# Batch norm with ReLU on one core: the stores of two neighbouring 4 MB pieces made one transfer from one tile

The kernel runs on one NeuronCore of a Trainium2 chip (the other cores stay idle). The metric is the device time of one execution in microseconds (us), where lower is better. The "span" of a profile is a little shorter: it was 81.9 us in a run of 83.77 us. The pieces of 1, 2, 4 and 8 MB are counted in units of 1024 x 1024 bytes, so a piece of 4 MB is 4.19 of the profile's MB.

## The reference, cut to what matters

```
x: (32, 128, 32, 32) float32;  gamma, beta, running_mean, running_var: (128,) float32;  eps = 1e-5
normalized = (x - running_mean[c]) / sqrt(running_var[c] + eps)
out = maximum(normalized * gamma[c] + beta[c], 0)          # float32
```

Every element is read once (16.78 MB) and written once (16.78 MB). With scale = gamma / sqrt(var + eps) and bias = beta - mean x scale, the arithmetic is one activation, relu(scale x + bias), for each row of a channel.

## The kernel before

The (batch, channel) rows are laid out as two halves (t = 0, 1) of 128 partitions with 16 rows of 1024 elements (4 KB) in each partition. A partition's 16 rows lie next to each other in memory (64 KB), and the halves lie 8 MB apart. Each piece has a block of on-chip memory, a tile. SyncE loads the pieces, ACT (ScalarE) activates them in place, and ACT issues the stores:

```python
PIECES = (((0, 2), (2, 4), (4, 8), (8, 16)), ((0, 8), (8, 16)))
STORE_CUTS = {(0, 1)}
...
for t in range(T):
    for a, b in PIECES[t]:
        xt = data.tile([P, b - a, HW], F32, name=f"x{t}_{a}")
        nc.sync.dma_start(out=xt, in_=xr[t, :, a:b, :])
        tiles.append((t, a, b, xt))
# ... four tiny parameter loads on ACT's queue, then scale_t and bias_t [P, 16] (cut)
for t, a, b, xt in tiles:
    first = a
    for j in range(a, b):
        nc.scalar.activation(out=xt[:, j - a, :], in_=xt[:, j - a, :], func=ACTF.Relu,
                             bias=bias_t[:, j : j + 1], scale=scale_t[:, j : j + 1])
        if j + 1 == b or (t, j + 1) in STORE_CUTS:
            nc.scalar.dma_start(out=outr[t, :, first : j + 1, :],
                                in_=xt[:, first - a : j + 1 - a, :])
            first = j + 1
```

So there are six loads (1, 1, 2, 4, 4, 4 MB) and seven stores (0.5, 0.5, 1, 2, 4, 4, 4 MB).

Of the kernel before, what the change touches and what calls it, by code (L numbers as in the profile page):

```python
# [1 line left out]

# [4 lines left out]


F32 = mybir.dt.float32
ACTF = mybir.ActivationFunctionType  # L10



J = 16

PIECES = (((0, 2), (2, 4), (4, 8), (8, 16)), ((0, 8), (8, 16)))

STORE_CUTS = {(0, 1)}


@with_exitstack
def kernel(
    ctx: ExitStack,
    tc: tile.TileContext,
    x: bass.AP,
    gamma: bass.AP,
    beta: bass.AP,
    running_mean: bass.AP,
    running_var: bass.AP,
    eps: bass.AP,  # L30
    out: bass.AP,
):
    nc = tc.nc
    B, C, H, W = x.shape
    HW = H * W
    P = nc.NUM_PARTITIONS
    assert C % J == 0 and P % (C // J) == 0 and (B * C) % (P * J) == 0
    Q = C // J
    T = B * C // (P * J)

    xr = x.rearrange("b c h w -> (b c) (h w)").rearrange("(t p j) w -> t p j w", p=P, j=J)
    outr = out.rearrange("b c h w -> (b c) (h w)").rearrange("(t p j) w -> t p j w", p=P, j=J)

    data = ctx.enter_context(tc.tile_pool(name="data", bufs=1))
    params = ctx.enter_context(tc.tile_pool(name="params", bufs=1))
    psum = ctx.enter_context(tc.tile_pool(name="psum", bufs=1, space=bass.MemoryType.PSUM))

    tiles = []
    for t in range(T):
        for a, b in PIECES[t]:  # L50
            xt = data.tile([P, b - a, HW], F32, name=f"x{t}_{a}")
            nc.sync.dma_start(out=xt, in_=xr[t, :, a:b, :])  # L52
            tiles.append((t, a, b, xt))



    raw = params.tile([Q, 4, J], F32, name="raw")
    for k, src in enumerate((running_var, gamma, running_mean, beta)):
        nc.scalar.dma_start(out=raw[:, k, :], in_=src.rearrange("(q j) -> q j", j=J))
    eps_t = params.tile([P, 1], F32, name="eps_t")  # L60
    nc.vector.memset(eps_t, float(eps))  # L61
    rep = params.tile([Q, P // Q, Q], F32, name="rep")
    nc.gpsimd.memset(rep, 1.0)  # L63
    nc.gpsimd.affine_select(  # L64
        out=rep,
        in_=rep,
        compare_op=mybir.AluOpType.is_equal,
        fill=0.0,
        base=0,
        pattern=[[0, P // Q], [-1, Q]],  # L70
        channel_multiplier=1,
    )
    cols = psum.tile([P, 4, J], F32, name="cols")
    nc.tensor.matmul(  # L74
        cols.rearrange("p k j -> p (k j)"),
        rep.rearrange("q r s -> q (r s)"),
        raw.rearrange("q k j -> q (k j)"),
        start=True,
        stop=True,
    )  # L80
    std_t = params.tile([P, J], F32, name="std_t")
    nc.scalar.activation(out=std_t, in_=cols[:, 0, :], func=ACTF.Sqrt, bias=eps_t[:, 0:1], scale=1.0)  # L82
    rstd_t = params.tile([P, J], F32, name="rstd_t")
    nc.vector.reciprocal(out=rstd_t, in_=std_t)  # L84
    scale_t = params.tile([P, J], F32, name="scale_t")
    nc.vector.tensor_mul(out=scale_t, in0=cols[:, 1, :], in1=rstd_t)  # L86
    ms_t = params.tile([P, J], F32, name="ms_t")
    nc.vector.tensor_mul(out=ms_t, in0=cols[:, 2, :], in1=scale_t)  # L88
    bias_t = params.tile([P, J], F32, name="bias_t")
    nc.vector.tensor_sub(out=bias_t, in0=cols[:, 3, :], in1=ms_t)  # L90

    with tc.manual_schedule(engines={mybir.EngineType.Activation}):
        for t, a, b, xt in tiles:
            first = a
            for j in range(a, b):
                nc.scalar.activation(  # L96
                    out=xt[:, j - a, :],
                    in_=xt[:, j - a, :],
                    func=ACTF.Relu,
                    bias=bias_t[:, j : j + 1],  # L100
                    scale=scale_t[:, j : j + 1],
                )
                if j + 1 == b or (t, j + 1) in STORE_CUTS:
                    nc.scalar.dma_start(
                        out=outr[t, :, first : j + 1, :], in_=xt[:, first - a : j + 1 - a, :]
                    )
                    first = j + 1


# [1 line left out]
_INS = ['x', 'gamma', 'beta', 'running_mean', 'running_var', 'eps']  # L111
_OUTS = [((32, 128, 32, 32), 'float32')]

_NUMBERS = {'eps': 1e-05}


# [26 lines left out]
```

## Time and profile before

| | before |
|---|---|
| time, median of the first 3 runs | 83.94 us (83.83 to 84.08) |
| span of the profiled run | 81.9 us |
| ACT busy | 38.5 us, 47% |
| packets of loads + packets of stores and parameters, share of the 16 DMA engines | 48.4% + 47.8% |
| bytes | 33.56 MB, 410 GB/s over the span |

The share of the DMA engines is the number to read first: the two queues together fill 96% of the span. The prediction below shows these lines and reads them.

### The profile page before, as it was taken

How to read it: one execution, taken by the hardware profiler on the slowest of the kernel's cores; microseconds unless marked ns; L12 is line 12 of the kernel's file. 1: busy time of each engine (PE TensorE's matmuls, PEld its weight loads, DVE VectorE, ACT ScalarE, POOL GpSimd, SP SyncE). 2: the span in 40 equal slices, each digit the busy share in tenths (PEclk: the TensorE clock that was granted, in tenths of full speed). 3: DMA queues.
4: the chain of work that ended last, by engine and by line, in shares of the span. 5: the costliest groups of instructions: out<-in, count | busy, mean ns of one | idle time of the engine just before them, and what ended most of it. 6: DMA issues, size and time to landing. Idle time of an engine off the chain costs nothing.

```text
span 81.9 us, 119 instructions
## 1 busy us (share of the span) xinstructions
PE 0.7 (1%) x2; PEld 0.5 (1%) x2; DVE 0.8 (1%) x5; ACT 38.5 (47%) x34; POOL 0.8 (1%) x6
## 2 busy tenths in 40 slices
PE   0002000000000000000000000000000000000000
PEld 0002000000000000000000000000000000000000
DVE  0000300000000000000000000000000000000000
ACT  0600377799039999199994199993000000000000
POOL 3000000000000000000000000000000000000000
DMA  2899999989899999979789798996999899799690
GB/s 32 328 425 472 408 448 448 512 352 494 370 448 416 446 418 396 500 296 600 320 380 580 304 464 384 512 512 288 480 512 400 368 512 448 320 512 496 272 512 0
DMA packets 1936, 33.56 MB, mean 410 GB/s; under 512 B 272, under 2 KB 272, under 8 KB 528
## 3 DMA queue, kind: packets, MB, share of 16 engines
q1 hardware_dynamic: 864, 16.78, 48.4%
q10 hardware_dynamic: 1072, 16.78, 47.8%
HBM read 16.78 MB, written 16.78 MB: 410 GB/s over the span
## 4 chain that ended last, share of the span: by engine, by line
DMA 56%; ACT 11%; SPq 0%; issue 0%
DMA x<-in_x_dram 56%; ACT x L96 11%; SPq L52 0%
## 5 line engine op out<-in xcount | busy, mean ns | idle before, releaser
L96 ACT ACTIVATE x<-x,bias_t,scale_t 128x1024 f32<-128x1024 f32 x32 | 37.0, 1228 | 10.3 <-DMA x<-in_x_dram 7.9
L82 ACT ACT_TABLE_LOAD x1 | 1.3, 1283 | 2.6 <-issue 2.6
L82 ACT ACTIVATE std_t<-cols,eps_t 128x16 f32<-128x16 f32 x1 | 0.3, 273 | 4.5 <-PE cols L74 4.5
L74 PE MATMUL cols<-raw,rep 8*128 8x64 f32 x2 | 0.7, 428 | 7.7 <-DMA raw<-in_beta_dram 7.7
L74 PEld LDWEIGHTS cols<-raw,rep 8*128 8x128 f32 x2 | 0.5, 304 | 7.7 <-issue 7.7
L64 POOL TENSOR_SCALAR_AFFINE_SELECT rep<-rep 8x128 f32<-8x128 f32 x1 | 0.4, 392 | 0.1
L84 DVE RECIPROCAL rstd_t<-std_t 128x16 f32<-128x16 f32 x1 | 0.3, 254 | 7.8 <-ACT std_t L82 7.8
L63 POOL MEMSET rep<- 8x128 f32 x1 | 0.2, 195 | 0.3 <-POOLq L124 0.3
L86 DVE TENSOR_TENSOR scale_t<-cols,rstd_t 128x16 f32<-128x16 f32 x1 | 0.2, 175 | 0.1
L90 DVE TENSOR_TENSOR bias_t<-cols,ms_t 128x16 f32<-128x16 f32 x1 | 0.2, 175 | 0.0
L88 DVE TENSOR_TENSOR ms_t<-cols,scale_t 128x16 f32<-128x16 f32 x1 | 0.2, 175 | 0.0
L124 POOL MEMSET const-bfloat16-1.0<- 128x1 bf16 x1 | 0.1, 106 | 0.0
L124 POOL MEMSET const-uint8-127<- 128x1 uint8 x1 | 0.1, 106 | 0.0
L124 POOL MEMSET const-float32-0.0<- 128x1 f32 x1 | 0.1, 103 | 0.3 <-issue 0.3
L124 POOL MEMSET const-float32-1.0<- 128x1 f32 x1 | 0.1, 103 | 0.0
L61 DVE MEMSET eps_t<- 128x1 f32 x1 | 0.1, 59 | 0.9 <-PEq L124 0.9
## 6 DMA issues: line engine op xcount, KB each, us to landing
x<-in_x_dram SPq DMA_DIRECT2D x3, 4096.0 KB, 38.8
out_dram<-x ACTq DMA_DIRECT2D x3, 4096.0 KB, 27.9
x<-in_x_dram SPq DMA_DIRECT2D x2, 1024.0 KB, 5.7
x<-in_x_dram SPq DMA_DIRECT2D x1, 2048.0 KB, 11.2
out_dram<-x ACTq DMA_DIRECT2D x1, 2048.0 KB
out_dram<-x ACTq DMA_DIRECT2D x2, 512.0 KB, 18.8
out_dram<-x ACTq DMA_DIRECT2D x1, 1024.0 KB
raw<-in_running_var_dram ACTq DMA_DIRECT2D x1, 0.5 KB
```

Source lines behind the costliest of these rows:

```text
L61: nc.vector.memset(eps_t, float(eps))
L63: nc.gpsimd.memset(rep, 1.0)
L64: nc.gpsimd.affine_select(out=rep, in_=rep, compare_op=mybir.AluOpType.is_equal, fill=0.0, base=0, pattern=[[0, P // Q], [-1, Q]], channel ...
L74: nc.tensor.matmul(cols.rearrange("p k j -> p (k j)"), rep.rearrange("q r s -> q (r s)"), raw.rearrange("q k j -> q (k j)"), start=True, s ...
L82: nc.scalar.activation(out=std_t, in_=cols[:, 0, :], func=ACTF.Sqrt, bias=eps_t[:, 0:1], scale=1.0)
L84: nc.vector.reciprocal(out=rstd_t, in_=std_t)
L86: nc.vector.tensor_mul(out=scale_t, in0=cols[:, 1, :], in1=rstd_t)
L88: nc.vector.tensor_mul(out=ms_t, in0=cols[:, 2, :], in1=scale_t)
L90: nc.vector.tensor_sub(out=bias_t, in0=cols[:, 3, :], in1=ms_t)
L96: nc.scalar.activation(out=xt[:, j - a, :], in_=xt[:, j - a, :], func=ACTF.Relu, bias=bias_t[:, j : j + 1], scale=scale_t[:, j : j + 1],)
L124: nc = _bacc.Bacc("TRN2", target_bir_lowering=False, num_devices=1)
```

## The change

The tile of the first half's rows 8 to 15 and the tile of the second half's rows 0 to 7 become one tile with two parts. Each part is loaded and activated as before, but they are stored by a single transfer after the second part. That makes one transfer, one issue and one completion (a tiny packet on each of the 16 engines, as the packet counts show) less, with larger transfers; in exchange the first part's store is ready later.

```diff
-PIECES = (((0, 2), (2, 4), (4, 8), (8, 16)), ((0, 8), (8, 16)))
-STORE_CUTS = {(0, 1)}
+TILES = (((0, 0, 2),), ((0, 2, 4),), ((0, 4, 8),), ((0, 8, 16), (1, 0, 8)), ((1, 8, 16),))
+STORE_CUTS = {(0, 0)}
...
+    for pieces in TILES:
+        n = len(pieces)
+        rows = pieces[0][2] - pieces[0][1]
+        xt = data.tile([P, n, rows, HW], F32, name=f"x{pieces[0][0]}_{pieces[0][1]}")
+        for i, (t, a, b) in enumerate(pieces):
+            nc.sync.dma_start(out=xt[:, i], in_=xr[t, :, a:b, :])
+        tiles.append((pieces, xt))
...  (activations as before, on xt[:, i, j - a, :]; single pieces are stored as before)
+            if len(pieces) == 2:
+                (t0, a, b), (t1, c, _) = pieces
+                pitch = ((t1 - t0) * P * J + c - a) * HW
+                nc.scalar.dma_start(
+                    out=bass.AP(tensor=outr.tensor, offset=outr[t0, :, a:b, :].offset,
+                                ap=[[J * HW, P], [pitch, 2], [HW, b - a], [1, HW]]),
+                    in_=xt)
```

More of the change, by code (lines that the diff above doesn't have):

```diff
@@ L48 @@
     tiles = []
-    for t in range(T):
-        for a, b in PIECES[t]:
-            xt = data.tile([P, b - a, HW], F32, name=f"x{t}_{a}")
-            nc.sync.dma_start(out=xt, in_=xr[t, :, a:b, :])
-            tiles.append((t, a, b, xt))
+    for pieces in TILES:
[5 more added lines that the diff above has]
+        tiles.append((pieces, xt))
     raw = params.tile([Q, 4, J], F32, name="raw")
@@ L92 @@
     with tc.manual_schedule(engines={mybir.EngineType.Activation}):
-        for t, a, b, xt in tiles:
-            first = a
-            for j in range(a, b):
-                nc.scalar.activation(
-                    out=xt[:, j - a, :],
-                    in_=xt[:, j - a, :],
-                    func=ACTF.Relu,
-                    bias=bias_t[:, j : j + 1],
-                    scale=scale_t[:, j : j + 1],
-                )
-                if j + 1 == b or (t, j + 1) in STORE_CUTS:
-                    nc.scalar.dma_start(
-                        out=outr[t, :, first : j + 1, :], in_=xt[:, first - a : j + 1 - a, :]
-                    )
-                    first = j + 1
+        for pieces, xt in tiles:
+            first = 0
+            for i, (t, a, b) in enumerate(pieces):
+                for j in range(a, b):
+                    nc.scalar.activation(
+                        out=xt[:, i, j - a, :],
+                        in_=xt[:, i, j - a, :],
+                        func=ACTF.Relu,
+                        bias=bias_t[:, j : j + 1],
+                        scale=scale_t[:, j : j + 1],
+                    )
+                    if len(pieces) == 1 and (j + 1 == b or (t, j) in STORE_CUTS):
+                        nc.scalar.dma_start(
+                            out=outr[t, :, a + first : j + 1, :], in_=xt[:, 0, first : j + 1 - a, :]
+                        )
+                        first = j + 1 - a
+            if len(pieces) == 2:
+                (t0, a, b), (t1, c, _) = pieces
+                pitch = ((t1 - t0) * P * J + c - a) * HW
+                nc.scalar.dma_start(
+                    out=bass.AP(
+                        tensor=outr.tensor,
+                        offset=outr[t0, :, a:b, :].offset,
+                        ap=[[J * HW, P], [pitch, 2], [HW, b - a], [1, HW]],
+                    ),
+                    in_=xt,
+                )
 _INS = ['x', 'gamma', 'beta', 'running_mean', 'running_var', 'eps']
```

## The prediction

What the text says of the hardware can be looked up in the trace of the kernel before:

- The 435 GB/s is 4.19 MB in the 9.65 us between the two landings (61.65 and 71.30 us).
- From 24 to 44 us the loads and the stores have 240 packets each, with 7.34 and 1.18 MB.
- The packets of the stores start in the order of the issues: those of 4 KB from 14.6 us, of 8 KB from 36.6, of 16 KB from 46.4 and of 32 KB from 51.2 us. So nothing of the store issued at 33.05 us moved before 51.2 us.
- A completion packet took 0.009 us. A packet of 32 KB took 1.213 us, one of 16 KB 0.611 and one of 4 KB 0.159; eight of 4 KB are 1.27 us, 5% more than one of 32 KB (the text's "some per cent").

> **What bounds the kernel now.** I read the page first (busy shares, the 40 slices, the queue table), then the chain of waits, then the transfers in single stretches of time, then the timeline of ScalarE (ACT). The page:
>
> ```profile
> span 81.9 us, 119 instructions
> ...
> PE 0.7 (1%) x2; PEld 0.5 (1%) x2; DVE 0.8 (1%) x5; ACT 38.5 (47%) x34; POOL 0.8 (1%) x6
> ...
> DMA  2899999989899999979789798996999899799690
> ...
> q1 hardware_dynamic: 864, 16.78, 48.4%
> q10 hardware_dynamic: 1072, 16.78, 47.8%
> HBM read 16.78 MB, written 16.78 MB: 410 GB/s over the span
> ```
>
> ACT, the only busy compute engine, works 47% of the span. The packets of the two queues (q1: the loads, issued by SyncE; q10: the parameters and the stores, issued by ACT) take 48.4 + 47.8 = 96.2% of the time of all 16 DMA engines, 78.8 of 81.9 us. The row of slices shows where the rest is: the first slice (2) and the last two (9, then 0). So the kernel is bound by moving 33.56 MB, and what a change is worth is decided by whether it alters the bytes, the rate, or the time for which the engines stand empty.
>
> The chain that ended last tells less than it seems to:
>
> ```profile
> 7.99 38.77 DMA x<-in_x_dram
> 46.76 0.03 issue
> 46.79 9.16 ACT x L96 x8
> ```
>
> It ends with the last eight activations at 55.95 us, though 26 us of the span are still to come: the stores after them are followed by no instruction, so the chain doesn't count them. It must not be read as "the loads and ACT set the end". The stretches show it. First the timeline of ACT around the two stores concerned, then the queues from 0 to 44 us, from 46.8 to 81.9 us and from 80.5 us on:
>
> ```profile
> 33.05 0.34 ACTq L104 DMA_DIRECT2D out_dram<-x  x1
> 34.81 9.16 ACT L96 ACTIVATE x<-x,bias_t,scale_t 128x1024 f32<-128x1024 f32 x8 [1.79 <-DMA x<-in_x_dram]
> 44.00 0.34 ACTq L104 DMA_DIRECT2D out_dram<-x  x1
> 46.79 9.16 ACT L96 ACTIVATE x<-x,bias_t,scale_t 128x1024 f32<-128x1024 f32 x8 [2.82 <-DMA x<-in_x_dram]
> 55.97 0.34 ACTq L104 DMA_DIRECT2D out_dram<-x  x1
> ```
>
> ```profile
> q1 hardware_dynamic: 832, 16.25, 87.3%
> q10 hardware_dynamic: 432, 1.71, 9.4%
> ```
>
> ```profile
> q10 hardware_dynamic: 560, 14.42, 95.2%
> ```
>
> ```profile
> DMA packets 4, 0.00 MB, mean 0 GB/s; under 512 B 4, under 2 KB 4, under 8 KB 4
> ```
>
> By 44.0 us the stores had moved 1.71 MB, but 4.19 MB of stores (0.52 + 0.52 + 1.05 + 2.10) had been issued by 20.57 us. So 4.19 - 1.71 = 2.48 MB of older stores still stood in front of the store issued at 33.05, not one byte of which can have moved. That store landed at about 33.05 + 28.6 = 61.7 us (28.6 is the longest time to landing among the seven stores), the one of 44.00 at 44.00 + 27.3 = 71.3 us: 9.6 us apart, which is 4.19 MB at 435 GB/s. From 46.8 us on there are only stores, 14.42 MB of them, and the engines are full until the last data packets end before 80.5 us; after that there are four tiny completion packets. The first of the two stores thus starts near 61.7 - 9.7 = 52 us, the second near 61.7, the last near 71.3.
>
> [...] the packet counts are those of one packet for each partition of each transfer and one for each engine's completion (q1: 6 transfers x (128 + 16) = 864; q10: 7 x 144 = 1008, and 4 parameter loads x 16 = 64, together 1072). [...]
>
> [...] 430, 437 and 427 GB/s in the stretches 64 to 72, 72 to 78 and 46.8 to 56 us. [...]
>
> [...]
>
> [...] The merged store writes for each partition two runs of 32 KB that lie 8 MB less 32 KB apart. No run of before shows such a pattern; I take it up as a rival.
>
> **The change part by part.** The loads are the same six transfers in the same order, from the same engine with the same waits; only the destination of two of them is now one tile. The order of the instructions in the built program confirms that. Of the 32 activations none is added or removed; before the 17th to 24th and the 25th to 32nd the waits on their loads stay.
>
> (1) Removed: the store at 33.05 us, 0.34 us of ACT's queue. ACT then waited 1.79 us for a load anyway (until 34.81), so the 0.34 us lie in idle time: 0 us on the path.
>
> (2) Moved: 4.19 MB of store become ready at 44.00 instead of 33.05 us, 10.95 us later. They are not needed before about 52 us, since the queue serves 2.48 MB of older stores first, between 44.0 and 52. Slack: 52 - 44 = 8 us. Cost 0 us.
>
> (3) Merged: an 8.39 MB store at 44.00 with 2 x 128 runs of 32 KB. At 435 GB/s it takes 19.3 us, as the two did (9.6 + 9.6): 0 us. It should land where the second landed, at 71.3 us, with the last store behind it: the last is issued at 55.97 as before, 15 us ahead of its turn.
>
> (4) Completions: one transfer less is one completion packet less on each engine. The completions of before are 17 transfers on 16 or 8 engines, all among the 272 packets under 512 B; even at the whole 3.1 us that the queues leave unused they could not take more than 3.1 / 17 = 0.2 us each, and as tiny packets far less. Estimate, from 4 of them taking 0.2% of the 1.4 us stretch on all 16 engines: 0.002 x 1.4 x 16 / 4 = 0.01 us each. Gain about 0.01 us, and some hundredths more if the two runs of a partition go as one packet.
>
> (5) Waits by reuse of semaphores: the built program has eight for its transfers in turn, so one store less shifts who waits for whom. Before, the store at 44.00 also waited for the very first store; now the last store, at 55.97, does. The first store was issued at 10.99 and landed 14.2 us later, at 25.2 us. 0 us.
>
> The issue of the merged store may take longer than 0.34 us. ACT has 2.82 us of idle before the load of 46.76 is there, so up to 2.4 us more are free. Sum: 0 to -0.1 us on 83.94 us.
>
> **The rivals.** *Starvation*: the store of the first half's last rows leaves 11 us later, and the DMA engines run dry. For it: 4.19 MB are held back in a kernel bound by its transfers. If it happened without any backlog it would cost at most what the stores would have carried from 33.05 to 44.00; in the stretch 33 to 44 us the queue of the stores moved 0.79 MB, that is 0.79 MB / 435 GB/s = 1.8 us, to 85.8 us. Against it: all 0.79 MB are of older stores, and 2.48 MB of those are left at 44.0. I give it 1%.
>
> *Gain by coalescing*: one transfer of 8 MB instead of two of 4, one fixed cost saved. For it: the profile has time to landing of 27 us for these stores, which looks expensive. Against it: these are queueing times; between the stores' landings lie 9.6 us, no more than the bytes take. If each transfer left a gap of 1 to 2 us on the engines, the time would go to 82 or 83 us; but the stretch 46.8 to 56 us, with a change of transfer in it, is full to 99.3%. I give a gain over 2% (below 82.3 us) 1%.
>
> *Slower writes*: alternating between two regions 8 MB apart, or runs cut into smaller packets. Cut to 4 KB, each packet might cost some per cent more, about 1 us of 19.3, still within 2%. [...] Against it: [...] the last dimension stays 32 KB contiguous in the built program, and before, loads and stores in distant regions took turns at 431 GB/s (34 to 40 us). I give over 2% slower 2%.
>
> **Range and chances.** The sum is 0 to -0.1 us. Three runs of before lie from 83.83 to 84.08 us, so the spread of 0.1 to 0.2 us is larger than the effect, and another chip may add as much. Predicted 83.9 us; range 83.6 to 84.3 us. Chances: faster by over 2% 0.01, within 2% 0.97, slower by over 2% 0.02.
>
> **What would show it right or wrong.** Right: the page lists one store of 8192 KB, about 27 us from issue to landing, and two of 4096 KB fewer; q10 has 1056 packets (1072 - 16; 928 if two runs make one packet of 64 KB); its share stays near 47.8%; from 46.8 us on it again has 14.4 MB left at 95%; ACT's last group starts at 46.8 us. Wrong by starvation: the queue of the stores moves less than 0.7 MB from 33 to 44 us, or the slices between 44 and 56 us fall below 9. Wrong by coalescing: the same bytes from 51 to 80 us in visibly less time, and a share of q10 well below 47.8%. Wrong by slower writes: its share rises, and a stretch such as 56 to 64 us falls below 400 GB/s.

## The result

| | before | after |
|---|---|---|
| median (6 runs each, same rounds) | 83.92 us | 83.98 us |
| lowest to highest | 83.83 to 84.08 | 83.85 to 84.08 |

The ratio is 1.0002 with a 95% interval of 0.9989 to 1.0015: no difference. (A ratio here and below is the mean time of one kernel's fast runs over the mean of the other's fast runs of the same rounds, so not quite the ratio of the medians quoted.)

The page of the changed kernel, first the busy share of the DMA engines in 40 slices and the queues, then the issues (tile, engine, count, size, us from issue to landing):

```profile
span 81.9 us, 118 instructions
...
DMA  1999996979899898979799799997998899799690
...
q1 hardware_dynamic: 864, 16.78, 48.6%
q10 hardware_dynamic: 1056, 16.78, 47.8%
...
out_dram<-x ACTq DMA_DIRECT2D x1, 8192.0 KB, 27.3
out_dram<-x ACTq DMA_DIRECT2D x1, 4096.0 KB, 24.9
```

The queue of the stores has lost exactly the 16 completion packets of one transfer (1072 - 1056), and its share is the same 47.8%. The timeline of ACT around the merged store:

```profile
34.88 9.16 ACT L100 ACTIVATE x<-x,bias_t,scale_t 128x1024 f32<-128x1024 f32 x8 [1.79 <-DMA x<-in_x_dram]
44.06 0.39 ACTq L116 DMA_DIRECT2D out_dram<-x  x1
46.89 9.16 ACT L100 ACTIVATE x<-x,bias_t,scale_t 128x1024 f32<-128x1024 f32 x8 [2.85 <-DMA x<-in_x_dram]
56.08 0.35 ACTq L108 DMA_DIRECT2D out_dram<-x  x1
```

The store at 33.05 us is gone, and all else on ACT stands within 0.11 us of where it stood. The merged store lands at 44.06 + 27.3 = 71.4 us; before, the second of the two landed at 71.3 us. The queues from 46.8 to 81.9 us:

```profile
DMA packets 544, 14.42 MB, mean 411 GB/s; under 512 B 48, under 2 KB 48, under 8 KB 48
## 3 DMA queue, kind: packets, MB, share of 16 engines
q10 hardware_dynamic: 544, 14.42, 95.2%
```

That is the same 14.42 MB left at 46.8 us, at the same 95.2%, as before. From 33 to 44 us, while the first part's store was withheld, the queue of the stores moved 0.79 MB, as it did before:

```profile
q1 hardware_dynamic: 129, 3.70, 78.0%
q10 hardware_dynamic: 129, 0.79, 17.1%
```

### The profile page after: what moved, and what is told of

It is laid out like the page before. It is cut to its first block, busy times and chain, and to the rows that moved or that the text cites. A ratio compares the mean times of both kernels' runs of the same rounds, so it can differ in the third digit from the quotient of the medians.

```text
span 81.9 us, 118 instructions
## 1 busy us (share of the span) xinstructions
PE 0.7 (1%) x2; PEld 0.5 (1%) x2; DVE 0.8 (1%) x5; ACT 38.5 (47%) x34; POOL 0.8 (1%) x6
## 2 busy tenths in 40 slices
DMA packets 1920, 33.56 MB, mean 410 GB/s; under 512 B 256, under 2 KB 256, under 8 KB 512
## 3 DMA queue, kind: packets, MB, share of 16 engines
q1 hardware_dynamic: 864, 16.78, 48.6%
q10 hardware_dynamic: 1056, 16.78, 47.8%
HBM read 16.78 MB, written 16.78 MB: 410 GB/s over the span
## 4 chain that ended last, share of the span: by engine, by line
DMA 56%; ACT 10%; issue 2%; SPq 0%
DMA x<-in_x_dram 56%; ACT x L100 10%; SPq L55 0%
## 6 DMA issues: line engine op xcount, KB each, us to landing
out_dram<-x ACTq DMA_DIRECT2D x1, 8192.0 KB, 27.3
```

## The experiments

The theory has three parts. First, the later issue is hidden, because older stores keep the DMA engines supplied until about 52 us. Second, merging is worth nothing, because the engines do not pause between transfers (before, they are full to 99.3% from 46.8 to 56 us, with a change of transfer in it). Third, the write pattern of the merged store costs nothing. The rivals: a cost of the delay and a gain of the merge that cancel; a fixed cost for each transfer; and a slower write of two regions far apart. The 1 to 2 us that the record gives to a fixed cost is the rival's assumption. In the trace of the kernel before a lone start and end come to 1.4 us: 1.0 from the issue of the first load (0.81 us) to its first packet (1.84) and 0.4 from the last completion packet of the last store (80.60) to its landing (80.97). Whether the engines stand empty for such a time between transfers is what was tested. Twelve kernels ran, all correct.

### A first try at separating the delay from the merge: delay_only

```diff
 # the changed kernel, after both parts' activations
-                nc.scalar.dma_start(out=bass.AP(... both parts ...), in_=xt)
+                for i, (t, a, b) in enumerate(pieces):
+                    nc.scalar.dma_start(out=outr[t, :, a:b, :], in_=xt[:, i])
```

> The changed kernel with its merge undone and its delay kept: both 4 MB stores are issued one after the other at about 44 us. Theory (the delay is hidden behind the queue, and the merge is worth nothing): 83.9 us, ratio to before within 0.2%; the two stores land about 9.7 us apart, near 61.7 and 71.3 us. Rival (the delay costs up to 1.8 us and the merge pays it back, so that the two cancel in the changed kernel): 84.5 to 85.8 us here.

Measured: 83.91 us against 83.82, ratio 1.0006 (0.9994 to 1.0018). The number is as the theory expects, but the run did not do what it was to do. The timeline of ACT in this run:

```profile
34.92 1.24 ACT L100 ACTIVATE x<-x,bias_t,scale_t 128x1024 f32<-128x1024 f32 x1 [1.80 <-DMA x<-in_x_dram]
34.95 0.34 ACTq L115 DMA_DIRECT2D out_dram<-x  x1
36.07 8.01 ACT L100 ACTIVATE x<-x,bias_t,scale_t 128x1024 f32<-128x1024 f32 x7
```

In the program the first store stands behind the second part's eight activations, yet it was issued at 34.95 us, as soon as the first of them could start. It depends only on the first part's activations, which were done. So the delay was 1.9 us instead of 11, and the run decides nothing about the delay.

### The same mistake three times: hold2, hold5, hold8

These were to issue the merged store after 2, 5 or 8 of the last eight activations, by its place in the program:

```diff
 # the changed kernel, in the loop over the last tile's rows (HOLD = 2, 5 or 8)
+                    if t == 1 and a == 8 and j + 1 - a == HOLD:
+                        nc.scalar.dma_start(out=bass.AP(... both parts ...), in_=held[1])
```

The 1.1 us that the expectations take for the start of a store are an estimate from the first load of the kernel before, which took 1.0 us from its issue to its first packet (0.81 to 1.84 us).

> The merged store held until two of the last eight activations are done, issued at about 49.1 us. Theory (slack until 51.6 - 1.1 = 50.5 us): 83.9 us, ratio within 0.3%. Rival (no slack beyond 44 us): 83.9 + 5.1 = 89.0 us.

> The merged store held until five of the last eight activations are done, issued at about 52.6 us. Theory (the queue is empty from 51.6 us, first packets 1.1 us after the issue): 83.9 + 52.6 + 1.1 - 51.6 = 86.0 us (85.4 to 86.6). Rival (no slack beyond 44 us): 83.9 + 8.6 = 92.5 us. Rival (slack to 56 us and more): 83.9 us.

> The changed kernel with its merged store held until all activations are done, about 56.0 us, with nothing else new. Theory (the older stores run out at about 51.6 us, and a store put on an empty queue starts about 1.1 us after its issue, an estimate from the first load of the kernel before): the engines stand empty for 56.0 + 1.1 - 51.6 = 5.5 us, time 83.9 + 5.5 = 89.4 us (88.5 to 90.2), with a gap in the slices there. Rival (there is much more slack than I read, or stores and their order never matter): 84 us. Rival (no slack at all beyond 44 us): 83.9 + 12 = 95.9 us.

Measured: 83.94, 83.93 and 84.01 us, against 83.87, 83.87 and 83.82 before (ratios 1.0011, 1.0008 and 1.002, with intervals 0.9992 to 1.0029, 0.9989 to 1.0027 and 1.0002 to 1.0038). At face value hold5 and hold8 refute the theory, which expected 86.0 and 89.4 us. The timeline of hold8 says otherwise:

```profile
46.84 1.24 ACT L102 ACTIVATE x<-x,bias_t,scale_t 128x1024 f32<-128x1024 f32 x1 [2.83 <-DMA x<-in_x_dram]
46.86 0.39 ACTq L112 DMA_DIRECT2D out_dram<-x  x1
47.98 8.01 ACT L102 ACTIVATE x<-x,bias_t,scale_t 128x1024 f32<-128x1024 f32 x7
```

Line 112 is the merged store. It comes after all eight activations in the program and was issued at 46.86 us, before seven of them had started (the last ended at 55.99 us); in the other two runs it went out at 46.91 and 46.93. It did not overtake the one in front of those seven: the store's data were ready at about 44.0 us, yet it left at 46.86, 0.02 us after that activation, whose load had just come, had started. In delay_only it was the same (34.95 after 34.92). So in these runs an activation that still waits for its load holds back the transfers behind it, and activations whose data are there do not. To make a transfer wait for a certain activation, its place in the program was not enough here; with a dependence on that activation it did wait (late8 below, issued at 57.05 us). These three runs therefore show one thing only: an issue at 46.9 us, 2.8 us later than in the changed kernel, costs at most 0.4%, the largest upper end. The interval of hold8 just misses 1, which is not explained.

### Real delays: late_two, late4, late8

Here the last row of the held tile is activated later, so that the store truly depends on a late activation. The number of activations stays the same.

```diff
 # late4 and late8: n = 4 or 8 (pair: the tile with two parts; last: the last tile)
-  pair part 1 rows 0..7; merged store; last rows 0..7; last store
+  pair part 1 rows 0..6; last rows 0..n-1; pair part 1 row 7; merged store; last rows n..7; last store
 # late_two: the first part's last row waits for the second part, then two single stores
-  pair part 0 rows 0..7; pair part 1 rows 0..7; merged store
+  pair part 0 rows 0..6; pair part 1 rows 0..7; pair part 0 row 7; store part 0; store part 1
```

> As the run that was to hold the merged store to the end, but with a real dependence: the last row of the held tile is activated after all eight rows of the last tile, so the merged store cannot be issued before about 46.85 + 9 x 1.145 + 0.1 = 57.2 us. No other work is added. Theory (older stores run out at 51.6 us, loads are finished at 46.5, a store on empty queues starts about 1.1 us after its issue): empty engines for 57.2 + 1.1 - 51.6 = 6.7 us, time 90.6 us (89.8 to 91.4), with low slices from 52 to 58 us. Rival (the time does not depend on when these stores are ready, as the runs that failed to hold it would suggest if taken at face value): 84 us.

Measured: 90.55 us against 83.90, ratio 1.0792 (1.0773 to 1.0811), against an expected 90.6. The page's row of slices (each 2.2 us), the timeline, and a view of single stretches (from:to, length, busy time of each engine, clock, share of the DMA engines, GB/s):

```profile
DMA  2899999989699698979799900099879999599990
```

```profile
46.73 10.29 ACT L97 ACTIVATE x<-x,bias_t,scale_t 128x1024 f32<-128x1024 f32 x9 [3.96 <-DMA x<-in_x_dram]
57.05 0.39 ACTq L123 DMA_DIRECT2D out_dram<-x  x1
```

```profile
51.70:53.60 1.90, 0.00 (x0) 0.00 (x0) 0.00 (x0) 1.90 (x3) 0.00 (x0) 1.00 0.00 0
...
58.40:80.00 21.60, 0.00 (x0) 0.00 (x0) 0.00 (x0) 0.00 (x0) 0.00 (x0) 1.00 1.01 435
```

The three zeros in the row are the hole that starvation makes. From 51.7 us no packet starts (the view counts a packet whole at its start; the last older ones, completions, started between 51.3 and 51.6 us). The first packets of the merged store started between 57.9 and 58.2 us, 0.8 to 1.2 us after its issue. After the hole the rate is 435 GB/s again, so the lost time is never made up.

> The same with the held row activated after four rows of the last tile: issue at about 46.85 + 5 x 1.145 + 0.1 = 52.7 us. Theory: 52.7 + 1.1 - 51.6 = 2.2 us of empty engines, 86.1 us (85.5 to 86.7), 4.5 us less than with the row after all eight: past the slack each us of delay costs one us. Rival: 84 us.

Measured: 86.10 us against 83.90, ratio 1.0265 (1.0247 to 1.0283), against an expected 86.1. The store was issued at 52.76 us. The two runs agree on where the slack ends: 52.76 less the 2.20 us it cost (86.10 - 83.90) is 50.56 us, and 57.05 less 6.65 us (90.55 - 83.90) is 50.40 us. So in this kernel a delay up to about 50.5 us is free, and after that it costs its full length: between the two runs 4.45 us more for an issue 4.29 us later.

> The delay without the merge, with a real dependence: the last row of the first of the two pieces is activated after the second piece, and then both 4 MB stores are issued one after the other at about 45.2 us. Theory: 83.9 us, ratio within 0.2%, the two stores landing about 9.7 us apart near 61.7 and 71.3 us. Rival (the delay costs up to 1.8 us and the merge of the changed kernel pays it back): 84.5 to 85.8 us.

Measured: 83.98 us against 83.90, ratio 1.0014 (0.9997 to 1.0032). This time the delay is real:

```profile
45.03 0.34 ACTq L121 DMA_DIRECT2D out_dram<-x  x1
45.41 1.47 ACTq L122 DMA_DIRECT2D out_dram<-x  x1
```

The two stores landed at 45.03 + 16.5 = 61.5 us and 45.41 + 25.8 = 71.2 us, where they land before the change. So the delay without the merge costs at most the 0.3% of the interval's upper end, and the rival with its 0.6 to 1.9 us is refuted: beyond these 0.3% there is no loss in the changed kernel for a gain of merging to pay back.

### Is a transfer more or less worth anything? split2 and split_rows

> The kernel before with each of the three last stores cut into two of 64 partitions, packets unchanged: three transfers more instead of one less. Theory (between two transfers the DMA engines do not pause; one more costs each engine one tiny packet): 83.9 to 84.0 us, ratio within 0.2%; from 46.8 us on the queue of the stores again has 14.4 MB at about 95%. Rival (each transfer has a fixed cost on the engines): at 1 to 2 us each, 87 to 90 us. If half the partitions do not spread evenly over the 16 engines it gets slower too, and the GB/s from 52 us on would show it.

```diff
 # the kernel before, the three last stores
-  nc.scalar.dma_start(out=outr[t, :, first : j + 1, :], in_=xt[:, first - a : j + 1 - a, :])
+  for p, q in ((0, 64), (64, 128)):
+      nc.scalar.dma_start(out=outr[t, p:q, first : j + 1, :], in_=xt[p:q, first - a : j + 1 - a, :])
```

Measured: 109.23 us against 83.82, ratio 1.3041 (1.2996 to 1.3085). Neither side expected that. Three stretches of this run:

```profile
56.00:64.00 8.00, 0.00 (x0) 0.00 (x0) 0.00 (x0) 0.00 (x0) 0.00 (x0) 1.00 0.97 217
...
60.00:80.00 20.00, 0.00 (x0) 0.00 (x0) 0.00 (x0) 0.00 (x0) 0.00 (x0) 1.00 1.05 249
80.00:100.00 20.00, 0.00 (x0) 0.00 (x0) 0.00 (x0) 0.00 (x0) 0.00 (x0) 1.00 0.98 244
```

All 16 engines are busy for over 90% of the time, but they move 217 to 249 GB/s, little more than half of the rate of the kernel before (437 from 56 to 80 us). So uneven spreading over the engines, the reason given, is not what happened. A gap between transfers would show as a low share, not as a low rate at a high share; here the packets themselves are slow: a store packet of 32 KB took 1.21 us before, and here 2.1 to 2.3 us on average, an estimate from the shares and rates of the three stretches (in the first, 0.97 of 16 engines for 8 us and 53 packets). Why they are slow was not shown; measured is only that the stores of 64 partitions each ran at 217 to 249 GB/s. As a test of the cost of a transfer the run is spoilt, so the cut was made along the rows:

```diff
 # the kernel before, the three last stores (pieces of 8 rows)
-  nc.scalar.dma_start(out=outr[t, :, first : j + 1, :], in_=xt[:, first - a : j + 1 - a, :])
+  for c, d in ((a, a + 4), (a + 4, b)):
+      nc.scalar.dma_start(out=outr[t, :, c:d, :], in_=xt[:, c - a : d - a, :])
```

> The kernel before with each of the three last 4 MB stores cut into two of 4 rows and all 128 partitions: three transfers more, packets of 16 KB instead of 32 KB. Theory (no pause between transfers; each packet more costs an engine about 0.01 us): per engine 3 x 8 more packets and 3 more completions, 27 x 0.01 = 0.3 us, time 83.9 to 84.2 us. Rival (a transfer has a fixed cost of 1 to 2 us on the engines): 87 to 90 us.

Measured: 84.00 us against 83.90, ratio 1.0014 (0.9996 to 1.0031). The page:

```profile
DMA  3899997979797979899799899999999999999990
...
q10 hardware_dynamic: 1504, 16.78, 47.9%
```

With 432 packets more (1504 - 1072: 3 x 128 of data and 3 x 16 completions) the share rises from 47.8 to 47.9%. Three transfers more cost at most the interval's upper end, 0.3% or 0.26 us, under 0.1 us each. A fixed cost of 1 to 2 us on the engines is refuted. In the other direction, one transfer less has nothing to give. Larger stores changed nothing beyond the interval, neither 4 MB instead of 2 MB here (1.0014) nor 8 MB instead of 4 MB in the change (1.0002). The 0.01 us for a packet more has its measure in the trace of the kernel before: two packets of 16 KB took 2 x 0.611 us, 0.009 us more than one of 32 KB.

### A longer delay and regions exactly 8 MB apart: far_pair

```diff
-TILES = (((0, 0, 2),), ((0, 2, 4),), ((0, 4, 8),), ((0, 8, 16), (1, 0, 8)), ((1, 8, 16),))
+TILES = (((0, 0, 2),), ((0, 2, 4),), ((0, 4, 8),), ((0, 8, 16), (1, 8, 16)), ((1, 0, 8),))
 # loads and activations keep their order; the pair is stored after its second part
```

> The store of the first half's last 8 rows is merged with that of the second half's last 8 rows, issued at about 56 us: it is delayed by 23 us instead of 11, and its two runs per partition lie exactly 8 MB apart. The store of the second half's first 8 rows goes alone at 44 us. Theory (order and age of stores do not matter while the queue holds others): 83.9 us, ratio within 0.2%. Rival 1 (a held-back store costs by the length of its delay): slower than before by some us. [...]

Measured: 83.95 us against 83.82, ratio 1.0016 (1.0004 to 1.0029). The issues:

```profile
out_dram<-x ACTq DMA_DIRECT2D x1, 8192.0 KB, 25.1
out_dram<-x ACTq DMA_DIRECT2D x1, 4096.0 KB, 17.7
```

The merged store was issued at 56.06 us, here behind a real dependence, and landed at 81.2 us. The other store, issued at 44.06, landed at 61.8, so the merged one took 19.4 us for 8.39 MB. So here runs exactly 8 MB apart were written at 432 GB/s, near the 437 of the stores before from 56 to 80 us, and the first part's store could wait for 23 us, while the other store, issued at 44.06 us, kept the queue supplied. The 0.1 us that the ratio resolves is not explained, and it is far below the "some us" of the first rival. The second rival, slower writing of such runs: the 432 GB/s refute it.

### No backlog of small stores: even_two and even_one

```diff
 # even_two: the kernel before with
-PIECES = (((0, 2), (2, 4), (4, 8), (8, 16)), ((0, 8), (8, 16)));  STORE_CUTS = {(0, 1)}
+PIECES = (((0, 8), (8, 16)), ((0, 8), (8, 16)));  STORE_CUTS = set()
 # even_one: the changed kernel with
+TILES = (((0, 0, 8),), ((0, 8, 16), (1, 0, 8)), ((1, 8, 16),));  STORE_CUTS = set()
```

> The kernel before with all loads and stores in four pieces of 4 MB and no small stores at the start, so all packets are of 32 KB and the two queues share the engines evenly: no backlog of small-packet stores builds up. It is the partner of the run that merges the middle two stores. Expected by working: the last load is near 60 us, the last store is issued near 69 us and is just in time; 83.9 us, perhaps up to 1 us more.

> The same four pieces of 4 MB, with the second and third store merged into one issued near 49 us. The first store has then been finished for some 8 us, so there is no backlog at all. Theory (held-back stores cost nothing as long as loads are waiting: they take the engines at full rate instead): the queue of the stores moves nearly nothing from about 42 to 49 us while the total stays near 430 GB/s; the last load comes near 50 us instead of 60; time 83.9 us, within 1% of its partner. Rival (a backlog of stores is needed; without it a delay costs its length): 7 to 8 us more than its partner, 91 us.

Measured: 85.04 us and 85.11 us, both against 83.87 (ratios 1.0133 and 1.015, with intervals 1.0116 to 1.0151 and 1.0132 to 1.0168). The merge makes no visible difference here either, 0.07 us between the medians. The queues from 46.6 to 50.6 us, first of even_two, then of even_one:

```profile
q1 hardware_dynamic: 32, 1.05, 60.6%
q10 hardware_dynamic: 34, 0.59, 34.3%
```

```profile
DMA packets 68, 1.70 MB, mean 426 GB/s; under 512 B 16, under 2 KB 16, under 8 KB 16
## 3 DMA queue, kind: packets, MB, share of 16 engines
q1 hardware_dynamic: 50, 1.64, 94.8%
q10 hardware_dynamic: 18, 0.07, 4.0%
```

Even sharing shows from 24 to 55 us in even_two: 7.34 MB of loads and 5.67 MB of stores, the first of them issued at 24.09 us. In even_one the stores have nearly nothing to move in these 4 us, and the loads take their place: 94.8% instead of 60.6%, at 426 GB/s in total. The last tile's activations started at 55.71 us instead of 57.23. So stores held back while loads are waiting are not lost time; the loads come earlier instead. My timing was off, though: the first store landed at 49.6 us and not near 42, so the stretch nearly without stores (two data packets, 0.07 MB) is about 4 us and not 7, and most of it lies after the merged store's issue at 47.17. The run shows the exchange, but it is a weaker test than planned. Why both are 1.2 us slower than the kernel before was not traced to its end; the first activation starts at 14.9 us instead of 9.72, because the parameters, loaded beside 4 MB pieces, come at 12.8 to 12.9 us instead of 7.7.

No experiment points to a version that beats both kernels. In both, the packets fill 96% of the span.

## Why the prediction was right, point by point

- *The bound.* Moving 33.56 MB through busy engines sets the time. Shown: the same bytes, shares and rates before and after, and in late8 time is lost exactly where a hole appears in the DMA row.
- *Step 1, the removed issue.* ACT's activations stayed where they were (34.88 and 46.89 us). Its 0.34 us lay in ACT's wait for a load. Shown by the timeline.
- *Step 2, the delay.* Free, as predicted; late_two shows it without the merge, far_pair for 23 us with another store in its place. The slack was put at 8 us, from 44 to 52. Its end is at about 50.5 us by late4 and late8, so 6.4 us after the issue at 44.06. The term left out of that sum is the time from the issue to the first packet, about 1 us in late8 (57.05 to between 57.9 and 58.2 us); the rest is the coarse 52, read from landings, since in late8 the last older packets started between 51.3 and 51.6 us. Counting bytes comes nearer: at 44.0 us 2.48 MB of older stores and 0.53 MB of loads (16.78 - 16.25) were left, 6.9 us at 435 GB/s, so the engines run dry near 51 us. The conclusion did not hang on it.
- *Step 3, the merge.* The merged store landed at 71.4 us, predicted 71.3. far_pair shows that the pattern of two regions can be written at 432 GB/s.
- *Step 4, completions.* 1056 packets as predicted, so the two runs of a partition stayed two packets. The gain of 0.01 us cannot be measured; split_rows bounds a transfer's cost below 0.1 us.
- *Step 5, reuse of semaphores.* The last store was issued at 56.08 us; the first store, for which it now also has to wait, had landed at 10.9 + 15.2 = 26.1 us. No wait appeared.
- *Why the stores fall behind.* The packets show it. From 33 to 44 us before, 129 of loads and 128 of stores started, with 3.70 and 0.79 MB: a load's packet there has 32 KB, a store's 4 or 8 KB.
- *The rival of starvation* was sized at up to 1.8 us for a kernel with no backlog. That working has a weak place: loads were queued until 46.8 us, and even_one shows that loads then took over the engines (94.8% of them). Without a backlog of stores the cost of holding a store to 44 us would probably have been less; this kernel has the backlog, so that is argued and not shown for it.

What stays open: ratios of 1.0014 to 1.002 in four kernels (late_two, split_rows, far_pair, hold8) with intervals that just touch or just miss 1, 0.1 to 0.2 us.

## What to carry to other kernels

When the two DMA queues fill 96% of the span, ask of a change whether it alters the bytes, lowers the rate (split2 did, to 217 to 249 GB/s, without a hole) or opens a hole. In these runs a later store was free as long as anything else was queued (late_two, far_pair), and then cost its full length (late4 and late8, 4.45 us for 4.29). Work out the backlog of both queues (bytes issued less bytes moved) at the moment concerned, divide it by the rate, and subtract the start of a transfer: about 1 us on empty queues here (late8), 3.6 us beside running loads (the first store of the kernel before, issued at 10.99 us, first packet at 14.64). In an experiment that delays a transfer, give it something to depend on and look up its issue in the timeline before you believe the time: four runs here delayed less than their programs said, three of them far less.
